# Seven products for eight in the projection of a hybrid recurrent layer

## The chip, the cores and the metric

The kernel runs on one core of a Trainium2 chip. Such a core has a matrix engine (TensorE, PE in the profile), a vector engine (VectorE, DVE), an engine for functions of one argument (ScalarE, ACT), a general one (GpSimd, POOL) and one that here only issues transfers (SyncE, SP). Each works through its own instructions in order; they meet at semaphores. Sixteen DMA engines move data between the memory of the device (DRAM) and the on-chip memory (SBUF); PE writes to accumulation banks (PSUM). The metric is the time on the device for one execution in microseconds, the median over runs.

## The reference

One layer over 2048 positions of width 1024. A normed and modulated input is projected to ten parts by one weight matrix of 1024 x 9216; two linear recurrences (HGRN2 and retention, 8 heads each) run on the parts; their normed outputs are gated, merged and projected back:

```python
h = rms_norm(x, norm_g[layer]) * (1.0 + scale) + shift
proj = h @ w_in[layer]
(hq, hf, hi, hz, rq, rk, rv, rz, ga, gb) = jnp.split(proj, offsets, axis=-1)
...
uA = head_rms_norm(oA, hg_norm_g[layer]) * jax.nn.silu(hz.astype(f32))
...
uB = head_rms_norm(oB, ret_norm_g[layer]) * jax.nn.silu(rz.astype(f32))
m = (jax.nn.sigmoid(ga.astype(f32)) * uA + jax.nn.sigmoid(gb.astype(f32)) * uB).astype(x.dtype)
x = x + gate * (m @ w_out[layer])
return rms_norm(x, final_g)
```

oA is the HGRN2 of hq, hf, hi: a state of 128 x 128 a head, with a decay that differs for each channel and position. oB is the retention of rq, rk, rv, whose q and k of 64 channels a head are rotated by position (rotary). All is in 32-bit floats.

## The kernel before

The positions go in two superblocks of 1024 (NSB = 2), the heads in four pairs (NP = 4). For each superblock and pair the function do_pair runs groups of products: "a" (f and q of the HGRN2, `gf` and `gq`, channels on the partitions), "b" for every second pair (q and k of the retention, `gr`, positions on the partitions), "c" (the values v of both, `gv`, positions on the partitions; they stay in SBUF as they are) and, for each of the two heads, "d" (`gg`: the four gate parts). Each group sums over the 1024 input channels in eight steps; each step is three matmuls of 128 x 128 x 512, since a 32-bit factor is split into a high and a low part and low times low is left out (mm3):

```python
PE.matmul(out=ps, lhsT=lh[0], rhs=rh[0], start=first, stop=False)
PE.matmul(out=ps, lhsT=lh[0], rhs=rh[1], start=False, stop=False)
return PE.matmul(out=ps, lhsT=lh[1], rhs=rh[0], start=False, stop=last)
```

All matmuls are issued at line 53, all transposes of PE at line 57, and PE keeps the order in which the program is written. Nothing is held from group to group but the split activations h (eight tiles for each block of 512 positions) and the weights: the class Ring loads a raw tile of two steps (L482, L480, on SP), splits it with ACT (the high part, L494) and DVE (the low part, L495) into one of 9 places (RING), 288 such splits in all.

Between the dense matmuls the recurrences run as generators in the class Background: after at least 9 steps of dense work (GAP) it lets each lane run one burst of small matmuls. The HGRN2 works with a tree over chunks of 16, 32, 64 .. 512 positions (`lv`, `poh`), the retention in chunks of 128 (`rt`, `por`). The q and k of the retention are rotated by DVE (L779, L793, L794), turned (L796) and sent through DRAM. normed (L706, L120, L121, L709) norms an output over its head; merge (L898, L901, L903) multiplies it with the gates (gates: L885, L888, L889), adds the two recurrences, turns the sum and stores it to mT_dram (L908).

startup works on h and the first v products at once. The last stage reads mT_dram, splits it (L1051, L1052), multiplies with the output weights (`ops`, 768 matmuls; load_wo, L1029 to L1031) and norms (L1239 to L1257). Which instruction of DVE, ACT, POOL and SP comes when is set by a scheduler that goes by dependences and priorities; only PE's order is the program's.

## Time and profile before

| what | us |
|---|---|
| median of 2 runs | 2048.34 |
| the two runs | 2047.32 and 2049.36 |
| the profiled execution, its own time and its span | 2048.5 |
| PE busy | 2029.8 |
| DVE busy | 1067.8 |
| ACT busy | 603.1 |
| POOL busy | 141.9 |

The span is the time from the first to the last instruction of the profiled execution; the profile gives no other time of that execution. An engine's busy time counts its arithmetic, not its issuing of transfers and its waits. Matmuls are pipelined and overlap in the record, so that a row's mean of one matmul is longer than the time it adds; that time is read where many follow each other without a gap. The DMA share is the mean busy share of the 16 DMA engines. A row of a window gives, for each engine, busy time and in brackets the instructions, then the clock that was granted to PE (1.00 is full), the DMA share and the rate in GB/s.

### The profile page before, as it was taken

To read this page: it belongs to the slowest core of one execution; us is meant where nothing else is said; L and a number is where in the kernel's file an instruction comes from. 1 tells how busy PE (TensorE), PEld (TensorE's weight loads), DVE (VectorE), ACT (ScalarE), POOL (GpSimd) and SP (SyncE) were. 2 spreads that over 40 slices of the span, in tenths; PEclk is the share of its full clock that TensorE was granted. 3 is DMA by queue.
4 is the path that set the end of the run, shared out by engine and by line. 5 is a ranking of instruction groups with operands and counts; after the bars stand their busy time and mean duration, and the time that the engine had idled before them with its cause. 6 is when DMAs were issued, how large, how long until landed. Compare 5 with 4: busy or idle time off the path is not lost.

```text
span 2048.5 us, 38333 instructions
## 1 busy us (share of the span) xinstructions
PE 2029.8 (99%) x15480; PEld 1672.5 (82%) x15480; DVE 1067.8 (52%) x2411; ACT 603.1 (29%) x1443; POOL 141.9 (7%) x246
## 2 busy tenths in 40 slices
PE   8999999999999999999999999999999999999998
PEld 6788888888888888888888888888878887888887
DVE  7376634553465535557465535553555535568432
ACT  7412222322114222436123212322123222323431
POOL 1000100110001100120000100010000100010000
PEclk9999999999999999999999999999999999999999
DMA  8135321322344211334334211321333211337541
GB/s 321 42 80 130 81 54 53 90 59 51 75 119 103 63 48 54 99 107 142 80 93 99 66 50 55 88 61 50 89 94 100 68 47 54 88 108 215 191 134 62
DMA packets 312562, 187.67 MB, mean 92 GB/s; under 512 B 217664, under 2 KB 274496, under 8 KB 312384
## 3 DMA queue, kind: packets, MB, share of 16 engines
q1 hardware_dynamic: 312384, 185.22, 32.9%
q8 instruction: 121, 1.98, 0.4%
q14 instruction: 57, 0.47, 0.1%
HBM read 147.39 MB, written 37.75 MB: 90 GB/s over the span
## 4 chain that ended last, share of the span: by engine, by line
PE 95%; DMA 2%; DVE 1%; ACT 1%; issue 0%; SPq 0%; POOL 0%; POOLq 0%; DVEq 0%; ACTq 0%
PE gg L53 34%; PE gv L53 16%; PE ops L53 9%; PE gq L53 9%; PE gf L53 8%; PE gr L53 8%; PE poh L53 4%; PE lv L53 3%; PE por L53 3%; PE rt L53 2%; DMA wc<-in_w_c_dram 1%; DVE wlc L495 0%; DMA bad<-in_bada_t_dram 0%; DVE wa L189 0%; DMA wd<-in_w_d_dram 0%
## 5 line engine op out<-in xcount | busy, mean ns | idle before, releaser
L53 PE MATMUL gg<-whd,h 128*128 128x512 f32 x2048 | 655.5, 394 | 0.0
L53 PEld LDWEIGHTS gg<-whd,h 128*128 128x128 f32 x2048 | 384.8, 188 | 77.9 <-issue 0.2
L53 PE MATMUL gg<-wld,h 128*128 128x512 f32 x1024 | 398.7, 389 | 0.0
L53 PE MATMUL gv<-whc,h 128*128 128x512 f32 x1024 | 330.4, 399 | 2.0 <-ACT h L393 1.9
L53 PEld LDWEIGHTS gv<-whc,h 128*128 128x128 f32 x1024 | 191.2, 189 | 43.6 <-ACT h L393 4.2
L53 PEld LDWEIGHTS gg<-wld,h 128*128 128x128 f32 x1024 | 192.6, 188 | 37.2 <-issue 0.2
L53 PE MATMUL gv<-wlc,h 128*128 128x512 f32 x512 | 194.3, 392 | 0.7 <-DVE wlc L495 0.7
L53 PE MATMUL gr<-whb,h 128*128 128x512 f32 x512 | 160.0, 391 | 0.0
L53 PE MATMUL ops<-wo,mh 128*128 128x512 f32 x512 | 157.9, 390 | 0.0
L53 PE MATMUL gq<-h,wha 128*128 128x512 f32 x512 | 157.7, 389 | 0.0
L53 PE MATMUL gf<-h,wha 128*128 128x512 f32 x512 | 157.6, 389 | 0.0
L885 ACT ACTIVATE sgg<-gg 128x512 f32<-128x512 f32 x128 | 75.5, 596 | 241.8 <-PE gg L53 241.3
L121 POOL TENSOR_TENSOR rrr<-ssr,mhalf 128x2 f32<-128x2 f32 x64 | 54.5, 851 | 1198.0 <-DVE ssr L120 1085.5
L495 DVE TENSOR_TENSOR wld<-wd,whd 128x512 fp32r<-128x512 f32 x128 | 86.3, 685 | 63.7 <-ACT whd L494 60.8
L53 PEld LDWEIGHTS gv<-wlc,h 128*128 128x128 f32 x512 | 96.6, 189 | 21.3 <-DVE wlc L495 2.2
L53 PEld LDWEIGHTS ops<-wo,mh 128*128 128x128 f32 x512 | 96.1, 188 | 20.3 <-DVE wo L1031 0.2
L53 PEld LDWEIGHTS gr<-whb,h 128*128 128x128 f32 x512 | 96.1, 188 | 20.0
L53 PEld LDWEIGHTS gf<-h,wha 128*128 128x128 f32 x512 | 96.1, 188 | 19.9
L53 PEld LDWEIGHTS gq<-h,wha 128*128 128x128 f32 x512 | 96.0, 188 | 19.8
L494 ACT ACTIVATE whd<-wd 128x512 fp32r<-128x512 f32 x128 | 79.2, 629 | 105.2 <-DMA wd<-in_w_d_dram 62.7
L888 DVE TENSOR_TENSOR ga<-gg,sgg 128x256 f32<-128x256 f32 x128 | 52.7, 415 | 94.0 <-ACT sgg L885 91.4
L53 PE MATMUL gr<-wlb,h 128*128 128x512 f32 x256 | 99.6, 389 | 0.0
(165 smaller groups left out, 2754.3 us busy)
## 6 DMA issues: line engine op xcount, KB each, us to landing
wd<-in_w_d_dram SPq DMA_DIRECT2D x64, 512.0 KB, 3.7
wc<-in_w_c_dram SPq DMA_DIRECT2D x32, 512.0 KB, 3.9
wa<-in_w_a_dram SPq DMA_DIRECT2D x32, 512.0 KB, 3.7
wa<-in_w_ada_dram SPq DMA_DIRECT2D x16, 512.0 KB, 7.6
wb<-in_w_b_dram SPq DMA_DIRECT2D x32, 256.0 KB, 3.2
qkT<-tr SPq DMA_DIRECT2D x128, 64.0 KB, 1.9
rqk<-qkT SPq DMA_DIRECT2D x64, 128.0 KB, 2.4
dk<-f SPq DMA_DIRECT2D x16, 512.0 KB, 2.8
```

What stands on the lines that cost most here:

```text
L53: made = nc.tensor.matmul(**kw)
L121: G.tensor_tensor(out=dst, in0=ss, in1=mhalf.broadcast_to([P, width]), op=ALU.pow)
L494: S.activation(out=hi, in_=w, func=AF.Copy)
L495: self.lasts.append(V.tensor_tensor(out=lo, in0=w, in1=hi, op=ALU.subtract).ins)
L885: S.activation(out=sg, in_=ps, func=AF.Sigmoid)
L888: V.tensor_tensor(out=ga, in0=ps[:, 0:256], in1=sg[:, 0:256], op=ALU.mult)
```

## The change

The projection is written anew. Columns go in quads: two blocks of 128 columns times two blocks of 512 positions, both with the two halves of the input channels; that is a product of 2 x 2 blocks, and Strassen's scheme (in Winograd's form) makes it of seven block products in place of eight. A quad is "a" (f, q of one head), "v" (the two v of one head), "b" (q and k of two heads of the retention), "A" or "B" (the gates of one); 36 for each superblock, 72 in all, and each product has 4 x 3 matmuls: 84 for a quad, 96 before.

- Activations: seven combinations of each of four channel blocks (A11, A12, A22, S1 to S4), split, are held in SBUF as 28 tiles. Those of the second superblock are made in the background by next_h, kept in DRAM and put in place by change_h around quad 36.
- Weights: four raw tiles are loaded for a quad, and one more that is summed up from step to step; the sums are made by DMAs that add to their destination, issued on POOL (Weights.add, L397, 4 for a quad, 288 in all). Each of the seven is split as before (L303 on ACT, L304 on DVE; 504 in all) into one of 3 places.
- Folds: after(m, q) takes the products' sums from PSUM: three copies by ACT (stash, L474) and three sums by DVE (L487 after product 1, L494 after 6, L498 after 7) for a quad. Products 1, 6, 7 and 4 of a quad use one bank after each other, 5 and 3 another; between two of these lies one other product (product_order).
- All ten parts come out with channels on the partitions. So both v are turned (take_v: L582 on DVE, then L587 to DRAM, read back at L826 and L914), the outputs of the recurrences are turned on their way back (L809, DRAM, L1005), the gates go through DRAM (L674, L1003), the merge follows there (L1015, L1018), and the rotation reads tables that tables() turns through DRAM at the beginning (L604 to L618: 128 transfers of 16 KB).
- The tree works on one head (NC = 8), the GAP is 8; normed squares on ACT; the states and norms go through DRAM as well. The opening computes the first two products of three quads while the combinations are made. The output stage is as before.

The core of the diff (new functions with a plus, the old product with a minus):

```diff
-    def mm3(ps, lh, rh, first, last):
-        PE.matmul(out=ps, lhsT=lh[0], rhs=rh[0], start=first, stop=False)
-        PE.matmul(out=ps, lhsT=lh[0], rhs=rh[1], start=False, stop=False)
-        return PE.matmul(out=ps, lhsT=lh[1], rhs=rh[0], start=False, stop=last)
...
-    def group_tok(sb, key, c, nm):
-        ps = dense_ps(f"{nm}_{sb * CH + c}")
-        for kt in range(KT):
-            tok_step(sb, key, c, ps, kt)
-        return ps
...
+def product_order():
+    made = [(5, 0), (3, 0)]
+    for i in range(NQ):
+        nxt = i + 1
+        if i + 1 < FIRST:
+            made += [(6, i), (5, nxt), (7, i), (3, nxt), (4, i)]
+        elif i < FIRST:
+            made += [(6, i), (2, nxt), (7, i), (5, nxt), (4, i)]
+        elif i + 1 < NQ:
+            made += [(1, i), (3, i), (6, i), (2, nxt), (7, i), (5, nxt), (4, i)]
+        else:
+            made += [(1, i), (3, i), (6, i), (7, i), (4, i)]
+    return made
...
+    def combine(h11, h12, h21, h22, use):
+        use("A11", h11)
+        use("A12", h12)
+        use("A22", h22)
+        V.tensor_tensor(out=h22, in0=h21, in1=h22, op=ALU.subtract)
+        use("S1", h22)
+        V.tensor_tensor(out=h21, in0=h11, in1=h21, op=ALU.subtract)
+        use("S3", h21)
+        V.tensor_tensor(out=h11, in0=h22, in1=h11, op=ALU.subtract)
+        use("S2", h11)
+        V.tensor_tensor(out=h12, in0=h12, in1=h11, op=ALU.add)
+        use("S4", h12)
...
+        def add(self, t, q, b, nm):
+            if ADMA:
+                nc.gpsimd.dma_start(out=as_src(t), in_=wsrc(q, b), accum_op=ALU.add)
+            else:
+                w = tmp(f"wt{nm}")
+                nc.sync.dma_start(out=as_src(w), in_=wsrc(q, b))
+                V.tensor_tensor(out=t, in0=t, in1=w, op=ALU.add)
...
+        def split(self, t):
+            m, q = seq[self.nsplit]
...
+            self.parts[m, q] = t
+            if m in (1, 2, 3, 7):
+                self.rfree += 1
+            elif m == 4:
+                self.zfree += 1
+                del self.z[q]
+            else:
+                self.add(src, q, 3 if m == 5 else 2, f"{m}n_{q}")
+            self.nsplit += 1
+            self.load()
...
+    def product_step(ps, m, q, j, first, last):
+        sb = QUADS[q][0]
+        at = combos[sb, ACOMBO[m], j]
+        bt = W.parts[m, q]
+        at_j = j % 2 * 2 + j // 2
+        ls = [z[:, at_j * P : (at_j + 1) * P] for z in bt]
+        for n, (x, y) in enumerate(((0, 0), (0, 1), (1, 0))):
+            PE.matmul(
+                out=ps, lhsT=ls[x], rhs=at[y], start=first and n == 0, stop=last and n == 2,
+                skip_group_check=True,
+            )
...
+    def stash(nm, ps):
+        t = upool.tile([P, 512], F32, name=nm, tag="cc", bufs=NCC)
+        S.activation(out=t, in_=ps, func=AF.Copy)
+        return t
...
+    def after(m, q):
+        with tc.high_priority(offset=PEV):
+            if m == 2:
+                c2s[q] = stash(f"c2_{q}", yb.pop(q))
+                return
+            if m == 5:
+                c5s[q] = stash(f"c5_{q}", vb[q])
+                return
+            if m == 1:
+                t = c2s.pop(q)
+                V.tensor_tensor(out=t, in0=xb[q], in1=t, op=ALU.add)
+                got = (0, 0, t)
+            elif m == 3:
+                c5s[q, 3] = stash(f"c53_{q}", vb.pop(q))
+                return
+            elif m == 6:
+                t = c5s.pop((q, 3))
+                V.tensor_tensor(out=t, in0=t, in1=xb[q], op=ALU.subtract)
+                got = (1, 0, t)
+            elif m == 7:
+                t = c5s.pop(q)
+                V.tensor_tensor(out=t, in0=t, in1=xb[q], op=ALU.subtract)
+                got = (1, 1, t)
+            else:
+                got = (0, 1, xb.pop(q))
+        deliver(q, *got)
...
+    def product(i):
+        m, q = seq[i]
+        if m == 2:
+            ps = yb[q] = bank(f"y{q}", xtag(q))
+        elif m == 1:
+            ps = xb[q] = bank(f"x{q}", xtag(q))
+        elif m == 5:
+            ps = vb[q] = bank(f"v{q}", "v")
+        elif m == 3:
+            ps = vb[q]
+        else:
+            ps = xb[q]
+        W.pump(i + NBW)
+        for j in range(4):
+            product_step(ps, m, q, j, m in (1, 2, 5) and j == 0, j == 3)
+            bg.tick(1.0)
+        W.parts.pop((m, q))
+        after(m, q)
...
+    def take_v(sb, h, s, tb, z):
+        y = tmp(f"vt{s}_{h}_{sb}_{tb}")
+        V.transpose(out=y, in_=z)
...
+                nc.sync.dma_start(out=t, in_=y)
+        yield
+        for b in range(L // BLK):
+            for i in range(2):
+                yield
+                for g in range(4):
+                    t = turned[i][(g // 2) * i]
+                    for j in range(4):
+                        nc.sync.dma_start(
+                            out=rot[i, b][32 * g : 32 * g + 32, :].rearrange("d (c j a) -> j d c a", j=4, a=32)[j],
+                            in_=t[32 * j : 32 * j + 32, b * P : (b + 1) * P].rearrange("d (c a) -> d c a", a=32),
+                        )
...
+    def opening():
+        was = {0: ada_load(0)}
+        scb = row_of_c()
+        W.load()
...
+        lower_bounds()
+        late_consts()
+        for _ in tables():
+            pass
+        for q in range(FIRST):
+            after(2, q)
+            if q == 0:
+                after(1, q)
```

In the opening, SP's order before has the weights of the next groups one after the other; names are destination and source, and `w` with a letter is a raw weight tile:

```order
L482 DMA wa_1_661<-in_w_a_dram 128x1024
L482 DMA wa_2_667<-in_w_a_dram 128x1024
L482 DMA wa_3_703<-in_w_a_dram 128x1024
L480 DMA wb_0_739<-in_w_b_dram 128x2x256 x2
L93 DMA m_802<-in_msk_dram 128x66
L480 DMA wb_1_789<-in_w_b_dram 128x2x256 x2
L480 DMA wb_2_1029<-in_w_b_dram 128x2x256 x2
L480 DMA wb_3_1046<-in_w_b_dram 128x2x256 x2
L482 DMA wd_0_1063<-in_w_d_dram 128x1024
L482 DMA wd_1_1079<-in_w_d_dram 128x1024
```

Now the tables (`rot`, from the turned tables `tabd`) stand there, and behind them the raw weight of product 5 of the third quad (`wz`), then those of its product 7 and of the fourth quad:

```order
L618 DMA rot_1_312<-tabd_0_811 128x1x32 x16
L618 DMA rot_1_316<-tabd_0_817 128x1x32 x8
L618 DMA rot_1_316<-tabd_1_820 128x1x32 x8
L618 DMA rot_2_313<-tabd_0_811 128x1x32 x16
L618 DMA rot_2_317<-tabd_0_817 128x1x32 x8
L618 DMA rot_2_317<-tabd_1_820 128x1x32 x8
L618 DMA rot_3_314<-tabd_0_811 128x1x32 x16
L618 DMA rot_3_318<-tabd_0_817 128x1x32 x8
L618 DMA rot_3_318<-tabd_1_820 128x1x32 x8
L419 DMA wz_1052<-in_w_b_dram 128x4x128
L411 DMA w_2_1058<-in_w_b_dram 128x4x128
L411 DMA w_3_1060<-in_w_d_dram 128x4x128
```

The 128 transfers of the tables have come in ahead of `wz`; 96 of them stand in these rows, the others in front.

On PE at that place the order is now as follows; x, y, v with a number are the banks of that quad, b5_2 the split weights of product 5 of quad 2 (counted from 0):

```order
L82 MATMUL x0_521<-A22_0_2_676,b4_0_1049 128x512 x3
L82 MATMUL x0_521<-A22_0_3_753,b4_0_1049 128x512 x3
L82 MATMUL x1_523<-S2_0_0_513,b6_1_1082 128x512 x3
L82 MATMUL x1_523<-S2_0_1_603,b6_1_1082 128x512 x3
L82 MATMUL x1_523<-S2_0_2_688,b6_1_1082 128x512 x3
L82 MATMUL x1_523<-S2_0_3_765,b6_1_1082 128x512 x3
L82 MATMUL v2_1153<-S1_0_0_505,b5_2_1100 128x512 x3
L82 MATMUL v2_1153<-S1_0_1_595,b5_2_1100 128x512 x3
L82 MATMUL v2_1153<-S1_0_2_680,b5_2_1100 128x512 x3
L82 MATMUL v2_1153<-S1_0_3_757,b5_2_1100 128x512 x3
```

Product 5 of quad 2, whose raw weight is that `wz`, is the ninth product after the opening's six, so 14 x 12 = 168 dense matmuls stand ahead of it.

In the middle of the first superblock PE had, in a group of v, steps of three matmuls with a burst of small ones between:

```order
L53 MATMUL gv3_2_7753<-whc120_7296,h0_0_217 128x512
L53 MATMUL gv3_2_7753<-wlc120_7297,h0_0_217 128x512
L53 MATMUL gv3_2_7753<-whc120_7296,h0_0_217 128x512
L53 MATMUL rt3_1_7761<-rqk3_1_7511 128x128 x2
L53 MATMUL rt3_1_7761<-v3_0_7724,rkz3_0_7508 64x128 x2
L53 MATMUL lv3_0_2_7771<-q3_0_7318,k3_0_7317 32x16 x64
L53 MATMUL por3_0_0_7764<-v3_0_7724,scm3_0_7647 128x128
L53 MATMUL por3_0_1_7765<-v3_0_7724,scm3_0_7647 128x128
L53 MATMUL gv3_2_7753<-whc121_7548,h0_1_259 128x512
L53 MATMUL gv3_2_7753<-wlc121_7549,h0_1_259 128x512
```

Now, around the gates quad 21, PE goes from product 2 of quad 22 to product 7 of quad 21, to product 5 of quad 22, to product 4 of quad 21:

```order
L82 MATMUL y22_6666<-A12_0_3_750,b2_22_6620 128x512 x3
L82 MATMUL x21_6577<-S3_0_0_509,b7_21_6640 128x512 x3
L82 MATMUL x21_6577<-S3_0_1_599,b7_21_6640 128x512 x3
L82 MATMUL x21_6577<-S3_0_2_684,b7_21_6640 128x512 x3
L82 MATMUL x21_6577<-S3_0_3_761,b7_21_6640 128x512 x3
L82 MATMUL poh4_0_6705<-vh4_0_0_6248,k4_0_5619 128x128
L82 MATMUL poh4_0_6705<-vh4_0_0_6248,af_113 128x128
L82 MATMUL v22_6718<-S1_0_0_505,b5_22_6667 128x512 x3
L82 MATMUL v22_6718<-S1_0_1_595,b5_22_6667 128x512 x3
L82 MATMUL v22_6718<-S1_0_2_680,b5_22_6667 128x512 x3
L82 MATMUL v22_6718<-S1_0_3_757,b5_22_6667 128x512 x3
L82 MATMUL x21_6577<-A22_0_0_501,b4_21_6689 128x512 x3
```

A product is 12 matmuls now, and the same bank `x21` is used by products 6, 7 and 4 with one product of the other quad between.

DVE before has at a like place, among the gates of head 4, splits, gates and merges of 256 and 128 columns:

```order
L756 SCALAR_TENSOR_TENSOR st5_114<-st5_114,tl2_0_6446,poh2_4_6834 128x128
L495 TENSOR_TENSOR wld109_6862<-wd13_2_6796,whd109_6861 128x512
L709 SCALAR_TENSOR_TENSOR v2_4_6118<-poh2_4_6834,rrh2_4_6844,gh0_2_5600 128x128 x2
L898 TENSOR_TENSOR ga4_4_6724<-ga4_4_6724,v2_4_6118 128x256
L495 TENSOR_TENSOR wld110_6878<-wd13_3_6822,whd110_6877 128x512
L901 TENSOR_TENSOR ga4_4_6724<-ga4_4_6724 128x128
L495 TENSOR_TENSOR wld111_6888<-wd13_3_6822,whd111_6887 128x512
L903 STREAM_TRANSPOSE ga4_4_6724<-ga4_4_6724 128x128
L888 TENSOR_TENSOR ga4_6_6905<-gg4_6_6784,sgg4_6_6903 128x256
L889 TENSOR_TENSOR ga4_6_6905<-ga4_6_6905,sgg4_6_6903 128x256
L888 TENSOR_TENSOR ga4_7_6910<-gg4_7_6785,sgg4_7_6908 128x256
L889 TENSOR_TENSOR ga4_7_6910<-ga4_7_6910,sgg4_7_6908 128x256
```

Now the fold L498 of quad 21 comes behind rotations of quad 20 (`ct`, `sw`), turning, gates (`c2_21`) and splits; between the fold L494 of that quad and the first row here stand eleven others, three of a merge (L1015 twice, L1018), six of rotation, a transpose and a split:

```order
L630 TENSOR_TENSOR sw1_2_1_6491<-c5_20_6177,sn1_2_1_6490 64x512
L632 TENSOR_TENSOR ct1_2_1_6489<-ct1_2_1_6489,sw1_2_1_6491 128x512
L634 STREAM_TRANSPOSE sw1_2_1_6491<-ct1_2_1_6489 128x512
L629 TENSOR_TENSOR sw0_2_1_6570<-x20_6260,sn0_2_1_6569 64x512
L630 TENSOR_TENSOR sw0_2_1_6570<-x20_6260,sn0_2_1_6569 64x512
L631 TENSOR_TENSOR ct0_2_1_6568<-x20_6260,ct0_2_1_6568 128x512
L661 TENSOR_TENSOR c2_21_6468<-c2_21_6468,sz0_4_0_6617 128x512
L632 TENSOR_TENSOR ct0_2_1_6568<-ct0_2_1_6568,sw0_2_1_6570 128x512
L673 TENSOR_TENSOR c2_21_6468<-c2_21_6468,c53_21_6638 128x512
L562 MEMSET f5_0_7006 128x2
L304 TENSOR_TENSOR b4_21_6689<-wz_21_6158,b4_21_6689 128x512
L498 TENSOR_TENSOR c5_21_6549<-c5_21_6549,x21_6577 128x512
```

Three folds a quad have come in, each of which a product of PE waits for.

1459 lines of the change are left out of this document (695 added, 764 removed).

## Prediction

> **What bounds the kernel now.** I read the page from the top: busy shares, the slices, the queues, the summary of the chain. After that I asked for the chain in order of time, and for windows.
>
> ```profile
> span 2048.5 us, 38333 instructions
> PE 2029.8 (99%) x15480; PEld 1672.5 (82%) x15480; DVE 1067.8 (52%) x2411; ACT 603.1 (29%) x1443; POOL 141.9 (7%) x246
> ...
> PE   8999999999999999999999999999999999999998
> ...
> DVE  7376634553465535557465535553555535568432
> ...
> PEclk9999999999999999999999999999999999999999
> DMA  8135321322344211334334211321333211337541
> ...
> q1 hardware_dynamic: 312384, 185.22, 32.9%
> ...
> PE 95%; DMA 2%; DVE 1%; ACT 1%; issue 0%; SPq 0%; POOL 0%; POOLq 0%; DVEq 0%; ACTq 0%
> ```
>
> TensorE (PE) is busy for 2029.8 of 2048.5 us, in nearly every slice to the top digit and at a full clock; the chain that ended last is 95% PE. Vector (DVE) stands at half, the DMA engines at a third. So a matmul that is taken out is worth its own duration, as long as no other engine comes late. The profiled execution took 2048.5 us, the median shown is 2048.34: the sum below is made against 2048.5 and needs no correction.
>
> What one dense matmul costs shows in the chain's last long piece, the output stage with nothing between its matmuls (start, duration, what):
>
> ```profile
> 1867.46 174.14 PE ops L53 x768
> ```
>
> 174.14 / 768 = 0.2267 us. (The page's mean of 394 ns for one instruction overlaps its neighbours.) A window of 100 us in which hardly anything but dense matmuls ran gives 100 / 440 = 0.227 too, with DVE at 46 us and the DMA engines at 0.34:
>
> ```profile
> 1400.00:1500.00 100.00, 99.52 (x440) 82.02 (x438) 46.49 (x92) 18.86 (x32) 0.00 (x0) 1.00 0.34 94
> ```
>
> **The change part by part.**
>
> *Products.* 6912 projection matmuls become 72 quads x 84 = 6048; the 768 of the output stage stay, and so do the small ones of the recurrences. -864 x 0.2267 = -195.9 us. The time that PE spends on dense work before is 7680 x 0.2267 = 1741 us; 2029.8 - 1741 - 10 (transposes and warm-up matmuls of the opening) = 279 us is the small work, which I carry over.
>
> *Vector work.* These rows give a price for each new kind (columns: line, engine, operation, tiles, shapes, count | busy us, mean ns | idle before):
>
> ```profile
> L495 DVE TENSOR_TENSOR wld<-wd,whd 128x512 fp32r<-128x512 f32 x128 | 86.3, 685 | 63.7 <-ACT whd L494 60.8 <-PE lv L53 2.8
> ...
> L898 DVE TENSOR_TENSOR ga<-ga,v 128x256 f32<-128x256 f32 x128 | 53.1, 417 | 1.2
> ...
> L796 DVE STREAM_TRANSPOSE tr<-qk 128x512 f32<-128x512 f32 x32 | 22.7, 710 | 0.8
> ...
> L1239 DVE TENSOR_TENSOR xo<-xo,ops 128x512 f32<-128x512 f32 x32 | 22.0, 686 | 54.1 <-PE ops L53 54.1
> ...
> L189 DVE CUSTOM_DVE_ANT_0 wa<-wa,scb,bad 128x1024 f32<-128x1024 f32 x16 | 20.2, 1281 | 2.1 <-DMA wa<-in_w_ada_dram 2.0
> ...
> L1255 DVE SCALAR_TENSOR_TENSOR xo<-xo,or,fgs 128x512 f32<-128x512 f32 x16 | 12.0, 752 | 10.7 <-POOL or L1253 10.7
> ...
> L494 ACT ACTIVATE whd<-wd 128x512 fp32r<-128x512 f32 x128 | 79.2, 629 | 105.2 <-DMA wd<-in_w_d_dram 62.7 <-PE gv L53 18.6 <-PE gg L53 17.5
> ```
>
> Splits: 504 instead of 288 at 0.685 (the new tile has 512 columns as well), +148 us. Folds, the sums of the products: 213 of 128x512 from PSUM, nearest the row of L1239 with 0.686, +146. Turning v and the outputs: 128 transposes at 0.71 (row L796), +91. Combinations of the activations, 32 x 0.685 = 22, and some 15 us net of rotation, gates and merge (the 128x256 merges of L898, 0.417, become 64 of 128x512, which I put at L1255's 0.752, and adds). Sum 1068 + 422 = 1490 us, about 75% of the new span. On the average that fits; DVE is in order, though, and each quad makes PE wait for three folds: product 6 writes over what L487 reads, product 7 over what L494 reads, product 4 over what L498 reads. Between lies one product of 12 matmuls, 2.7 us, which is four DVE instructions. DVE's order, whose end at this place is shown above, has 23 instructions after L494 up to L498 of quad 21, the gates quad behind a quad of retention q and k: 3 merges (2 x 0.752 + 0.685), 2 transposes (1.42), 17 others of 0.685 (11.6) and a short one, 15.3 us. PE has there products 2 of the next quad, 7, and 5 of the next quad, 36 x 0.2267 = 8.2 us, and little small work: about 7 us of waiting. There are 8 such places (one for each such quad) and the change of the activations in the middle; a part of each is caught by PE running behind DVE (one product). Bounds: 0 if the fold is always ahead, 8 x 7 + some 30 at the other quads = 86; I take 40 us, since most of the other quads have DVE work for 10 to 20 us against 20 to 23 us of PE. ACT gets 216 more splits and 213 stashes at 0.629 (its row L494), +270 us on 603 before gates and squares: half of the span, and a stash has a whole product to be done in, so I cost it at nothing; if ACT were late, the next to wait is PE at the bank of products 5 and 3.
>
> *Clock after a wait.* The trace has one wait in mid-stream, 2.26 us at 1705:
>
> ```profile
> 1705.00:1710.00 5.00, 2.74 (x90) 2.25 (x79) 2.73 (x4) 0.36 (x1) 0.00 (x0) 0.90 0.21 75
> 1710.00:1715.00 5.00, 5.00 (x18) 4.03 (x17) 2.68 (x5) 0.00 (x0) 0.00 (x0) 0.75 0.00 0
> 1715.00:1720.00 5.00, 5.00 (x155) 4.00 (x155) 2.29 (x4) 1.34 (x5) 0.00 (x0) 1.00 0.15 43
> ```
>
> The granted clock is 0.90 and 0.75 in two windows of 5 us and then 1.00 again: (0.10 + 0.25) x 5 = 1.75 us lost. Eight waits like it: 14 us; none and 50 are the bounds.
>
> *The opening.* Before, PE computes v of the first pair from the start:
>
> ```profile
> 0.00:20.00 20.00, 4.10 (x17) 3.10 (x18) 0.00 (x0) 1.00 0.90 350
> 20.00:40.00 20.00, 15.78 (x61) 10.59 (x60) 0.00 (x0) 1.00 1.03 409
> 40.00:60.00 20.00, 18.61 (x73) 12.76 (x72) 2.28 (x4) 1.00 0.24 65
> 60.00:80.00 20.00, 12.15 (x46) 7.59 (x44) 2.26 (x4) 1.00 0.35 107
> ```
>
> That is 17 + 61 + 73 + 46 = 197 dense matmuls in 80 us, and by then PE is full. Afterwards nothing dense runs until the activations' combinations exist. On DVE these need 16 x 1.281 (L189) + 28 splits x 0.685 + 16 combinations x 0.685 + 6 weight splits and the row of c, about 8 us: 20.5 + 19.2 + 11.0 + 8 = 59 us, which begin at some 5 us, so 64 us. Meanwhile PE has 72 matmuls. Then the rotary tables: L618 issues 128 DMAs of 16 KB, all on SP, and behind them on SP stands the load of the raw weight of product 5 of the third quad (L419), which PE reaches after 168 dense matmuls. The DMAs of 16 KB that before has (minimum, median, maximum of an issue in ns):
>
> ```profile
> L908 SPq DMA_DIRECT2D mT_dram<-ga x512: 302/430/1967, 207.3 to 1878.9; - x171
> ...
> DMA to landing us min/median/max: 1.4/1.5/4.5
> ```
>
> 128 x 0.43 = 55 us (0.302 would give 39, the 0.604 of the row below 77). 64 + 55 + 4 for the two tables = 123 us; then the load:
>
> ```profile
> L480 SPq DMA_DIRECT2D wb<-in_w_b_dram x32: 539/604/684, 69.1 to 1446.5; - x32
> ...
> DMA to landing us min/median/max: 3.0/3.2/3.9
> ```
>
> 3.2 us, as much for the accumulating DMA behind it, 1.3 for the split and some latency: PE goes on at about 132 us, with 6048 + 768 - 168 = 6648 dense matmuls before it: 6648 x 0.2267 = 1507, + 279 small, + 8 for the tail (the last outputs are turned and merged through DRAM; before, the tail behind PE is 7): 1926 us. If the tables were hidden, PE would go on from 72 matmuls at 70 us: 70 + 6744 x 0.2267 + 279 + 8 = 1886. Their only cover are weights loaded before them, and there are three raw tiles and two for sums.
>
> *Accumulating DMAs.* 288 of 256 KB in pieces of 512 bytes, issued by POOL. Before issues none from POOL and adds nothing in flight: their price isn't in the trace. The plain load of the same size (L480, just above) lands in 3.2 us, and by the code an accumulate has about three products, 8 us, from its issue to its split, so I cost its latency at nothing; at twice 3.2 us it is still covered. On POOL's queue the powers of the output norms (L181) now stand behind adds that wait for their load; what waits for those are outputs on their way to the merge, for which PE waits only at the end, so nothing again; as issues, 288 at the 0.604 of L480 are 174 us on a POOL that is busy for 142. For the engines' load I take two rows: in the opening the DMA engines are full and move 409 GB/s,
>
> ```profile
> 15.00:20.00 5.00, 4.94 (x25) 3.67 (x24) 4.96 (x10) 2.50 (x5) 0.00 (x0) 1.00 1.03 410
> 20.00:40.00 20.00, 18.05 (x81) 12.97 (x80) 17.66 (x37) 17.06 (x35) 1.66 (x1) 1.00 1.03 409
> ```
>
> so 1.03 x 16 / 410 = 0.0402 ns a byte and engine; on the page the mean packet has 185.22 MB / 312384 = 593 bytes and takes 0.329 x 2048.5 x 16 / 312384 = 34.5 ns, so 10.7 ns are fixed. The changed kernel moves 423 MB in 865 thousand packets (its 360 + 288 weight transfers, and v, outputs, gates, tables through DRAM): (865e3 x 10.7 + 423e6 x 0.0402) / 16 = 1640 us of each engine, 83% of 1985, if an accumulating packet costs what a copy costs. Bounds: that, and three times that. If counted twice, 147456 packets x 31.3 ns / 16 = 288 us come on top, 1930 in all. I take the copy's price, with the rest as rivals. SP's queue has 2269 issues for 1252, at 0.43 some 976 us, half of the span.
>
> **Sum.** 132 + 1507 + 279 + 8 = 1926, + 40 for folds + 14 for the clock = 1980; the change of the activations in the middle (28 splits within seven products, DVE 31 us against PE 26) adds 5: 1985 us.
>
> **The rivals.**
> 1. Stalls hidden: the folds come in time and the tables hide partly. 1886 to 1930. For it: DVE at 75% leaves room. Against: the 23 instructions at each of eight places.
> 2. The DMA engines become the bound, each accumulating packet costing two. 1930 us of work on engines that can't be full in the opening (66 us idle or so) and at the tail: 2000 to 2080, say 2045, no measurable change. For it: 83% by the copy's price leaves little. Against: nothing in the rows but that weights are loaded in time at 33%. The mechanism is that an add reads its destination as well as its source. The Trainium skill states this in "Collectives: The Full Stack", section "The bandwidth ceiling: the fold count and why AG ≠ RS ≠ AR": an add in the DMA path needs two source reads, and the reduce ran at half the rate of the copy. No run here shows it yet.
> 3. Slower: PE waits at each of the 216 folds. Place: L487, L494, L498, behind whatever DVE has in hand. Price: 1945 without stalls; two DVE instructions ahead of each beyond the 2.7 us cover, 1.37 x 216 = 296, give 2240; it decides from 0.67 us a fold, (2089 - 1945) / 216, one instruction. For it: DVE itself waits for ACT and PE in its order (before, L495 has 63.7 us of such waits in 128). Against: folds are emitted with a priority that moves them ahead.
> 4. Accumulating packets at three prices: 1640 + 577 = 2217 us of each engine, so 2250, slower. It takes over 2.4 prices to matter.
>
> **How the numbers follow.** About 2% is what a measurement of this kernel can tell from no change: faster is below 2007, slower above 2089. Chances: the forecast's case 0.36 (1930 to 2007), rival 1 0.12, rival 2 0.18 and larger stalls that stay within 2% 0.08, rival 3 0.18, rival 4 0.08. So faster 0.48, same 0.26, slower 0.26. The likeliest case gives 1985. The range from 1915 to 2130 leaves out half of rival 1 (0.06) and what of rivals 3 and 4 lies above (0.14); the forecast's own range is 1930 to 2007.
>
> **What would show it.** In the profile after: the mean of a dense matmul in the chain's output piece still 0.227; PE empty in slices 2 and 3, with SP's queue in L618 until about 123 us; DVE at 1450 to 1530 us; folds as the releaser of PE's idle time with about 40 us, at gates quads above all; PEclk below 9 only after such waits; the DMA share at 0.80 to 0.85 (1 would be rival 2 or 4, with PE or the split waiting for the accumulating DMAs). Wrong would be a PE idle time spread evenly over quads (rival 3), or waits for POOL's queue, whose issues no row of before prices.

## The result, and the profile after

The changed kernel takes 2655.81 us (median of 2651.90 and 2659.71) for 2048.34: a ratio of 1.2964, 95% interval 1.2916 to 1.3012. It is slower by 30%. The profiled execution's span is 2650.1 us.

The page of the changed kernel, the lines that answer to those of before (busy times, three rows of slices, the DMA queues, the chain by engine):

```profile
span 2650.1 us, 40994 instructions
PE 1998.0 (75%) x14648; PEld 1584.5 (60%) x14648; DVE 1365.1 (52%) x2647; ACT 937.6 (35%) x2340; POOL 618.2 (23%) x674
...
PE   4526997499856887488774998399857888497998
...
PEclk9758998799987998798887999699988899798999
DMA  8347787668776798699885788668786778577753
...
q1 hardware_dynamic: 752720, 348.08, 49.9%
q0 software_dynamic: 152064, 75.52, 23.6%
...
PE 16%; DMA 8%; DVE 4%; SPq 3%; issue 3%; POOL 1%; ACT 1%; POOLq 0%; DVEq 0%; ACTq 0%
```

PE does fewer products and yet is busy for 1998.0 us, at a mean clock below full, and stands idle for 652 us; the chain no longer runs along PE (16%) but through transfers, DVE, SP's queue and others, in pieces of a few microseconds. What PE waited for (microseconds in all, times, the longest):

```profile
PE y L82 <- DVE ct L631: 231.8, 7, 39.9
PE v L82 <- ACT b L303: 73.4, 6, 70.1
PE poh L82 <- DMA vh<-vd: 53.7, 10, 9.7
PE rt L82 <- DMA rqk<-rd: 46.1, 9, 11.2
...
PE poh L82 <- DMA k<-dk: 27.4, 7, 12.9
...
PE x L82 <- DVE c L487: 14.8, 13, 3.6
...
PE x L82 <- DVE c L498: 12.2, 6, 4.2
...
PE x L82 <- DVE c L494: 6.5, 6, 1.8
```

The folds, L487, L494 and L498, which the prediction had as the whole of the waiting, make 33.5 us. Seven waits for a row of the rotation, L631, make 231.8. Windows of the opening and of the stretch from there to the last part of the output stage (PE busy, PE's loads, DVE, ACT, POOL, granted clock, DMA share, GB/s):

```profile
0.00:200.00 200.00, 83.44 (x430) 59.95 (x431) 82.64 (x164) 68.63 (x114) 30.13 (x39) 0.77 0.53 128
200.00:2540.00 2340.00, 1811.40 (x13766) 1439.49 (x13765) 1240.17 (x2402) 838.17 (x2158) 582.07 (x624) 0.89 0.77 165
```

So PE is idle for 117 us in the first 200 and for 529 us after, at a mean clock of 0.77 and 0.89. Against the 1985 us forecast: in PE's timeline the 70 us wait of the opening ends at 183 us and not at 132 (+51); idle time after it is 529 us for 40 (+489); and the busy time of PE exceeds the 2029.8 - 195.9 = 1834 us of full clock by 164, for 14 (+150). Together 690, a little more than the 671 that are missing: PE's work in the opening at a slow clock is counted in two of them.

**One of the seven long waits, link by link.** PE's timeline (start, duration; in brackets the idle time before) at the retention quad 20 and the gates quad 21, the place whose order the prediction had counted:

```profile
770.41 2.94 PE L82 MATMUL x<-S,b 128*128 128x512 f32 x12
813.30 5.28 PE L82 MATMUL y<-A,b 128*128 128x512 f32 x12 [39.95 <-DVE ct L631]
```

The second row is product 2 of quad 22. It writes to the bank that quad 20 used last (the code gives even quads the bank x0), and there the rotation still has to read product 4 (L631 reads `x20`). DVE's timeline before that:

```profile
773.39 0.69 DVE L494 TENSOR_TENSOR c<-c,x 128x512 f32<-128x512 f32 x1 [0.92 <-PE x L82]
777.29 0.75 DVE L1015 SCALAR_TENSOR_TENSOR mg<-mg,gnt,mu 128x512 f32<-128x512 f32 x1 [3.21 <-DMA mu<-ud]
779.04 0.75 DVE L1015 SCALAR_TENSOR_TENSOR mg<-mg,gnt,mu 128x512 f32<-128x512 f32 x1 [1.00 <-DMA mu<-ud]
...
786.47 0.69 DVE L631 TENSOR_TENSOR ct<-c,ct 128x512 f32<-128x512 f32 x1 [2.47 <-DMA ct<-rot]
796.09 0.69 DVE L304 TENSOR_TENSOR b<-wz,b 128x512 fp32r<-128x512 f32 x1 [8.93 <-ACT b L303]
...
811.04 0.68 DVE L629 TENSOR_TENSOR sw<-x,sn 64x512 f32<-64x512 f32 x1 [11.37 <-DMA sn<-rot]
...
812.47 0.69 DVE L631 TENSOR_TENSOR ct<-x,ct 128x512 f32<-128x512 f32 x1
```

The fold L494 is done at 774. Then DVE waits in its row for a load of the merge (3.2 and 1.0 us), for a table (2.5), for a split's high part (8.9) and for another table (11.4), and L631 comes at 812.5: 39 us, of which some 27 are waiting. SP's issues in that time show why the loads were late:

```profile
752.91 0.61 SPq L1005 DMA_DIRECT2D mu<-ud  x1
765.36 1.13 SPq L639 DMA_DIRECT2D rd<-ct  x2
766.53 5.31 SPq L1005 DMA_DIRECT2D mu<-ud  x3
771.88 1.52 SPq L1003 DMA_DIRECT2D mg<-gd  x1
773.45 3.61 SPq L1005 DMA_DIRECT2D mu<-ud  x4
...
778.31 0.67 SPq L419 DMA_DIRECT2D wz<-in_w_d_dram  x1
...
798.95 1.07 SPq L639 DMA_DIRECT2D rd<-ct  x2
800.12 6.20 SPq L644 DMA_DIRECT2D kzd<-sw  x4
806.36 1.64 SPq L627 DMA_DIRECT2D ct<-rot  x1
808.05 0.43 SPq L628 DMA_DIRECT2D sn<-rot  x1
```

SP stands from 753.5 to 765.4 in the store L639 until DVE has rotated; behind it stand the merge's loads (L1005), behind these the table and the next `wz` (778.31). POOL waits for that weight and issues its adding transfer at 783.72 (below), and only at 795.4, 11.7 us later, can ACT split it. That split is what DVE waits 8.9 us for, so this link is the time of two transfers as well as SP's order. Until the split is made DVE doesn't finish the next rotation, and SP, standing in the store L639 of that rotation, issues nothing from 791.2 to 798.95. Behind that store the four stores L644 take 6.2 us to issue, and the last table (L628, 808.05) stands behind them. Two queues, each in order, wait for each other in turn. The DMA engines were not full: their share is 0.82 from 780 to 792, 0.15 from 792 to 800 and 0.60 from 800 to 812. POOL's row:

```profile
783.72 1.44 POOL L397 DMA_DIRECT2D wz<-in_w_d_dram  x1 [15.31 <-DMA wz<-in_w_d_dram]
```

DVE has the same four waits in the same order (merge load, table, split, table) ahead of the waits of PE that end at 531, 1438, 1725 and 2296; the one at 1997 has the last two of them, and the shortest, at 1112, another (a load of x, 12.4 us).

### The profile page after: what moved, and what is told of

Same layout as the page of the kernel before. It is cut to its first block, busy times and chain, and to the rows that moved or that the text cites. A ratio compares the mean times of both kernels' runs of the same rounds, so it can differ in the third digit from the quotient of the medians.

```text
span 2650.1 us, 40994 instructions
## 1 busy us (share of the span) xinstructions
PE 1998.0 (75%) x14648; PEld 1584.5 (60%) x14648; DVE 1365.1 (52%) x2647; ACT 937.6 (35%) x2340; POOL 618.2 (23%) x674
## 3 DMA queue, kind: packets, MB, share of 16 engines
q0 software_dynamic: 152064, 75.52, 23.6%
## 5 line engine op out<-in xcount | busy, mean ns | idle before, releaser
L82 PE MATMUL v<-S,b 128*128 128x512 f32 x1728 | 455.8, 409 | 88.3 <-ACT b L303 73.4
L82 PE MATMUL x<-S,b 128*128 128x512 f32 x1704 | 440.1, 403 | 25.7 <-DVE c L487 14.8
L82 PE MATMUL x<-A,b 128*128 128x512 f32 x1704 | 431.7, 403 | 20.7 <-DVE c L498 12.2
L82 PE MATMUL y<-A,b 128*128 128x512 f32 x852 | 248.4, 441 | 252.7 <-DVE ct L631 231.8
L82 PEld LDWEIGHTS v<-S,b 128*128 128x128 f32 x1728 | 332.6, 197 | 166.8 <-ACT b L303 76.8
L82 PEld LDWEIGHTS x<-S,b 128*128 128x128 f32 x1704 | 322.1, 193 | 103.2 <-ACT b L303 15.6
L82 PEld LDWEIGHTS x<-A,b 128*128 128x128 f32 x1704 | 322.7, 193 | 92.9 <-ACT b L303 9.4
L304 DVE TENSOR_TENSOR b<-w,b 128x512 fp32r<-128x512 f32 (+1 forms) x320 | 200.3, 635 | 257.5 <-ACT b L303 254.1
L304 DVE TENSOR_TENSOR b<-wz,b 128x512 fp32r<-128x512 f32 (+1 forms) x240 | 150.4, 636 | 309.6 <-ACT b L303 308.7
L397 POOL DMA_DIRECT2D wz<-in_w_d_dram x96 | 149.5, 1585 | 495.9 <-DVE b L304 338.7
L303 ACT ACTIVATE b<-w 128x512 fp32r<-128x512 f32 (+1 forms) x320 | 183.2, 584 | 189.2 <-PE x L82 82.0
L303 ACT ACTIVATE b<-wz 128x512 fp32r<-128x512 f32 (+1 forms) x240 | 137.5, 583 | 223.2 <-DMA wz<-in_w_b_dram 71.3
L82 PE MATMUL ops<-wo,m 128*128 128x512 f32 x768 | 179.7, 394 | 8.1 <-ACT m L303 4.7
L474 ACT ACTIVATE c<-v 128x512 f32<-128x512 f32 x144 | 85.7, 595 | 146.6 <-PE v L82 146.3
L397 POOL DMA_DIRECT2D wz<-in_w_a_dram x48 | 80.5, 1678 | 135.0 <-DVE b L304 85.4
L474 ACT ACTIVATE c<-y 128x512 f32<-128x512 f32 x71 | 42.3, 596 | 177.5 <-PE y L82 177.3
```

Source lines behind the costliest of these rows:

```text
L82: return tc.keep_in_program_order(nc.tensor.matmul(**kw))
L303: S.activation(out=t[0], in_=src, func=AF.Copy)
L304: return V.tensor_tensor(out=t[1], in0=src, in1=t[0], op=ALU.subtract)
L397: nc.gpsimd.dma_start(out=as_src(t), in_=wsrc(q, b), accum_op=ALU.add)
L474: S.activation(out=t, in_=ps, func=AF.Copy)
```

## The experiments

Each time is that of one execution; the kernel before, run beside them on the same chip, took 2047.9 to 2052.6. Differences are against 2655.8, whose two runs are 7.8 us apart; less than that is called no gain.

### Single links

**a1_copy.** Plain copies for the adding transfers:

```diff
-                nc.gpsimd.dma_start(out=as_src(t), in_=wsrc(q, b), accum_op=ALU.add)
+                nc.gpsimd.dma_start(out=as_src(t), in_=wsrc(q, b))
```

> The 288 transfers that add to their destination become plain copies of the same size from the same queue (POOL); the sums of the weights are left out. Theory SP (SP's single queue brings weights and rotary tables late): the time stays within 60 us of 2656, since the order and the issues are the same. Theory DMA (an adding packet costs two copies, so the DMA engines hold everything up): the queue of POOL falls from 23.6% of 2650 us to about 11%, landing from 6 us to about 3.5, and the time falls by 200 us or more.

2558.7 us, 97 less: between the two. POOL's queue on its page (packets, MB, share of 16 engines):

```profile
q0 software_dynamic: 23040, 75.52, 10.5%
```

0.105 x 2556.9 x 16 = 4296 us of engine time for the same 75.52 MB that cost 0.236 x 2650.1 x 16 = 10007 us when added: 2.3 times, or 65.8 ns for each of 152064 packets. The share is as theory DMA had it, and landing fell from 5.9 to 4.3 us in the median; the time is not as it had it: the waits for L631 are still 195 us. The edit changes more than the adding: the copies go in larger packets (23040 for 152064), and POOL issues one in 0.88 us for 1.45.

**a2_rot_act.** Loads of the tables from ACT (`nc.scalar.dma_start` at L627 and L628):

> The 64 loads of the rotary tables (L627, L628) are issued by ACT, not by SP. Theory SP order (the fourth load of a retention quad waits on SP behind the stores L644): the seven waits of the bank y for L631, 232 us, fall to under 80 and the time by 150 us or more. Theory tiles (the load waits for its place, whatever the queue): the waits stay within 60 us of 232 and the time within 60 of 2656.

2634.3, 22 less. The waits for L631 fell to 126 us, but 63 us for the tree's k through DRAM (27 before) and others came in their place. The fall of the waits lies between the two theories; the time is that of the second.

**a3_stash.** The fourth sum copied out of PSUM:

```diff
-                got = (0, 1, xb.pop(q))
+                z = xb.pop(q)
+                if QUADS[q][1] == "b":
+                    z = stash(f"c4_{q}", z)
+                got = (0, 1, z)
```

> ACT copies the fourth sum of a retention quad out of PSUM, so that the bank is free without DVE. Theory bank (the wait is for the bank alone): the 232 us of waits for L631 vanish, and the time falls by 200 us or more. Theory SP (DVE stands in its row behind a late table, and the folds behind it): the wait for L631 vanishes but comes back at L498 or at a split within two or three products; the time falls by 100 us at most.

2660.2, no gain. The bank is free, and PE waits at the same places a few rows later, for the tree's k, not at the fold or the split that the second theory named:

```profile
PE poh L82 <- DMA k<-dk: 208.4, 8, 35.9
```

So the bank is where the delay shows, not where it is made.

**a4_weights_act.** Weights loaded from ACT (`nc.scalar.dma_start` at L411 and L419):

> The 360 plain loads of weights (L411, L419) are issued by ACT, not by SP. Theory SP (weights are late because they stand behind the tables and the outputs on SP): the first long wait, 70 us at 113, falls to under 20, the waits for splits shrink, and the time falls by 150 us or more. Theory DMA (the engines are the bound): the time stays within 60 us of 2656. Against a gain: 360 x 0.6 us more on ACT's row.

2651.9, no gain; the waits for L631 are 240 us. The first long wait of 70 us went, but one of 55 for a turned v (L582) came just behind it. The first theory had the wait right and the time wrong. The second has the time, but the engines' load is not the whole of the loss either: a1_copy takes it down and gains 97 us.

**a5_tables.** Half of the tables later:

```diff
+            if b == NBLK:
+                yield "rest"
...
-        for _ in tables():
-            pass
+        tab = tables()
+        for said in tab:
+            if said == "rest":
+                break
+        bg.side.append(tab)
```

> In the opening only the 64 transfers of the rotary tables that the first superblock needs are issued; the other 64 come from the background later. Theory SP in the opening (the 70 us wait is the queue of tables ahead of the third quad's weights, 88 us for 128): the wait falls by 40 us or so, to about 27, and the time by 40 to 60. Theory other (the wait is for the sum that POOL makes, or for the split): the wait stays within 10 us of 70.

2657.0, no gain, but the scheduler had moved most of the later transfers up again. SP's row of the tables, of the kernel as changed and of this one:

```profile
93.50 80.08 SPq L618 DMA_DIRECT2D rot<-tabd  x122
```

```profile
95.51 70.26 SPq L620 DMA_DIRECT2D rot<-tabd  x106
```

16 fewer stood ahead of `wz`, and the wait fell from 70.1 to 60.2 us: 0.62 us for each. That fits a wait for the queue of tables, most of which the edit hadn't taken away; c1_tables32 below settles it.

**a7_bstores, a8_stores.** Stores of rotated q and k, and then all stores of results, from ACT (`nc.scalar.dma_start` at L639 and L644; at L587, L674, L784, L812, L883 and L1022 as well):

> The stores of the rotated q and k (L639, L644) are issued by ACT, the loads stay on SP. Theory convoy (SP and DVE are two queues in order that wait for each other: SP stands in a store until DVE has rotated, DVE stands in a row until SP has issued the load behind that store): the seven long waits, 232 us, fall to under 90 and don't come back elsewhere; the time falls by 130 us or more. Theory DMA (the transfers of these stretches take that long on the engines): the waits stay over 170 us, the time within 60 us of 2656.

> All stores of results to DRAM (L587, L639, L644, L674, L784, L812, L883, L1022, some 580 issues) are issued by ACT. Theory convoy: beside the long waits those for v and the rotated q and k (L826, L911, 100 us) shrink to about half; the time falls by 250 us or more. Against: ACT gets 350 us of issues in front of its splits; if that costs more than SP gains, the splits (L303) become PE's releaser and the time stays above 2560.

2604.1 and 2605.2, 52 and 51 less. The waits for L631 fell to 130 and 79, but with all stores on ACT the tree's k made 91 us and `lv` 42 us of new ones. Convoy's sign, but 52 where it had 130 or more, and 51 where it had 250 or more. The splits on ACT did not become what PE waits for (74 us, nearly all in the opening).

**a6_dve_add.** Sums on DVE:

```diff
-ADMA = True
+ADMA = False
```

> The sums of the weights are made on DVE from plain loads, with no adding transfers. DVE gets 288 x 0.685 = 197 us more, SP 288 issues. Theory DMA: the DMA share falls from 0.75 to about 0.62 and the time by 100 us or more. Theory convoy (more loads on SP and more rows on DVE make the waiting worse): the time rises by 100 us or more.

2616.9, 39 less, with the DMA share at 0.60. Neither theory. The waits for L631 fell to 106 us, but behind the opening PE waited 87 for splits on ACT (8 in the kernel as changed). So part of the gain went into later weights; whether DVE's longer row (1538 us) or SP's 288 more loads delayed them isn't shown.

### Several together

**b1_three.** The edits of a1_copy, a8_stores and a3_stash in one kernel.

> Three single edits together: plain copies for the adding transfers (the weights' sums are left out), all stores of results from ACT, and the fourth sum of a retention quad copied out of PSUM. Alone they gave 97, 51 and 0 us (2558.7, 2605.2, 2660.2 for 2655.8). Theory chain (a long wait is a row of links one behind the other, in queues that are in order: a link taken out gains its own length only, and the wait moves to the next): the gains add, about 150 us, 2500 to 2530. Theory bank and queue as single causes, hidden by each other: over 250 us.

2538.8, 117 less, where the single gains sum to 148. That is 9 us short of the chain's 2500 to 2530 and far from the 250 us of the other theory: the gains nearly add, and of these three none hid a large one.

**b2_no_rot, b3_rows.** Rotation without loads, and turned transfers in whole rows (shown for L1005; L587, L644 and L777 likewise):

```diff
-        nc.sync.dma_start(out=ct, in_=rot[0, b])
-        nc.sync.dma_start(out=sn, in_=rot[1, b])
+        sn = tb1 = combos[sb, "A11", 0][0]
```

```diff
-                        out=ut[32 * i : 32 * i + 32, :].rearrange("e (c j t) -> e c j t", c=4, j=4),
-                        in_=ud[s, h, b].rearrange("(j e) (c i t) -> i e c j t", j=4, c=4, i=4)[i],
+                        out=ut[32 * i : 32 * i + 32, :],
+                        in_=ud[s, h, b][32 * i : 32 * i + 32, :],
```

> The rotation reads a resident tile in place of its loaded tables (so q and k of the retention are not rotated); DVE's rows stay, 64 loads and two of twelve places in the ring of working tiles go. Theory loads of tables (the fourth load behind the stores sets the wait): the seven waits, 232 us, fall under 60, nothing takes their place, time 200 us or more lower. Theory chain: the wait is cut by the 14 us that the profile shows for the two loads in the stretch at 773 (2.5 and 11.4), the rest stays at a split or at k<-dk; the time falls by 80 to 150 us.

> The turned transfers (v, k of the retention, the tree's k, the outputs: L587, L644, L777, L1005) move whole rows of 2 KB in place of pieces of 128 bytes, as many issues and bytes, so that their results are not turned. Theory pieces (360 thousand of 905 thousand packets are these pieces; they fill the DMA engines and SP's issues): packets fall below 560 thousand, the DMA share from 0.75 to about 0.6, SP's issues of 1.4 to 1.8 us to 0.6, and the time by 150 us or more. Theory chain: the share falls likewise, but the time only by 50 to 100 us.

2566.6 (89 less, the chain's band, though the waits for this row of the rotation fell to 45 us: 78 for the tree's k and 44 for splits took their place) and 2470.2 (186 less, the largest single gain, in time the band of pieces). The second kernel's packets:

```profile
DMA packets 567067, 426.21 MB, mean 173 GB/s; under 512 B 59472, under 2 KB 469072, under 8 KB 566864
```

Only 59 thousand are under 512 bytes, for 420 thousand in the kernel as changed, while the DMA share fell just from 0.74 to 0.72 of a shorter span, not to 0.6; the store L644 took 0.48 us to issue in the median, for 1.41. So the gain is of the pieces, but whether through the engines or through SP's issues stays open. The seven waits for L631 are 159 us there.

**b4_all.** The edits of b2_no_rot, b3_rows and a1_copy in one kernel.

> Whole rows, plain copies and no table loads together (the weights' sums, the turning and the rotation are left out). PE, ACT and DVE keep their rows. Theory DMA (all that is lost is lost to transfers: their number, their adding, their place in the queue): the time falls to 2150 or less. Theory vector row (PE waits for DVE in its order even when transfers are quick): 2300 or more, with L487, L494, L498 and the splits as PE's releasers.

2354.7, 301 less where the three single gains sum to 372. Over the 2300 of the second theory, but not by its folds: besides the 69 us of the opening, PE's largest waits are 73 us for the tree's k and 39 for the retention's state (L957), both of the recurrences. So I asked what is left without them.

### The projection alone, the opening, a kernel with all that helped

**c2_core, c4_core_copy.** What a quad delivers is dropped but for a part of A; in the second kernel the adding transfers are copies too:

```diff
+        if kind == "A" and ch == 0:
+            if tb:
+                z = stash(f"c4_{q}", z)
+            nc.sync.dma_start(out=mT_dram[b][n], in_=z)
+            msent[n, b] = bg.now
...
-        if kind == "a":
-            take_a(sb, n, ch, tb, z)
```

> The recurrences, gates, turning and merge are left out: what a quad delivers is dropped, but for two parts of each quad A that are stored for the output stage. The opening, the weights with their adding transfers, splits, folds, the change of the activations and the output stage stay: 6816 dense matmuls, 1545 us. Theory recurrences (the projection keeps up by itself): 183 for the opening + 6648 x 0.2267 = 1690, + 10 for the tail, so 1690 to 1760, with PE at over 95% from 200 us on. Theory weights (the three places, the adding transfers and the folds are too slow by themselves): over 1850, with the splits as PE's releaser.

> As the kernel before it in this list, with plain copies in place of the adding transfers (the weights' sums left out too). Theory recurrences: within 20 us of that kernel. Theory weights: at least 60 us faster than it.

1759.0, the upper end of the first theory's range and 59 over its sum without waits, and 1734.8: the projection, with its folds, splits and adding transfers, nearly keeps up by itself. Page and a window of the first:

```profile
PE 1598.3 (91%) x6904; PEld 1308.4 (74%) x6904; DVE 684.0 (39%) x1131; ACT 582.0 (33%) x1075; POOL 449.9 (26%) x354
```

```profile
1000.00:1100.00 100.00, 100.00 (x443) 82.81 (x442) 36.08 (x58) 31.34 (x58) 30.67 (x22) 1.00 0.73 132
```

From 200 to 1700 us PE is busy for 1470 of 1500; in steady stretches 443 matmuls in 100 us, 0.226 us each, with the DMA engines at 0.73. The adding transfers cost 24 us here, a little more than the first theory's 20.

**c1_tables32.** Tables in 32 transfers (each for all four blocks):

```diff
-        for b in range(L // BLK):
...
+                        out=rot_all[i][32 * g : 32 * g + 32, :].rearrange("d (c j a) -> j d c a", j=4, a=32)[j],
+                        in_=t[32 * j : 32 * j + 32, :].rearrange("d (c a) -> d c a", a=32),
```

> The rotary tables are turned by 32 transfers of 64 KB in place of 128 of 16 KB; all else stays. Theory SP in the opening (in a5 the wait fell by 10 us with the 16 transfers that left the queue, 0.65 us each): 32 x 0.7 to 1.4 = 22 to 45 us on SP instead of 88, the wait of 70 us falls to 5 to 30, and the time by 45 to 65 us. Theory other: the wait stays within 10 us of 70.

2593.2, 63 less. The wait in the opening:

```profile
PE v L82 <- ACT b L303: 15.5, 5, 13.3
```

**c3_best.** The edits of c1_tables32, a8_stores and a3_stash, and `nf <= n + 2` for `nf <= n + 1` in the HGRN2's fetch of v.

> Everything is computed. Tables in 32 transfers, all stores of results from ACT, the fourth sum of a retention quad copied out of PSUM, and v of the HGRN2 fetched one chunk earlier. Theory chain (links add): 55 + 51 + 0 + 35, so about 2515. If the links hide each other: 2400 or less. It is not expected to reach the kernel before the change.

2544.5, 111 less than the kernel as changed, with everything computed. The parts sum to 114 (63 + 51 + 0) if the earlier fetch of v gave nothing. It doesn't reach the kernel before; no variant that computes everything did.

### One recurrence at a time

**d1_hgrn, d2_ret.** What the quads of one recurrence deliver is dropped (shown for the first):

```diff
+        if kind in ("b", "B"):
+            return
...
+        if s == 1:
+            return
```

> The retention is left out: its rotation, tables, v, gates and chunks; merge takes the HGRN2's part alone. The projection's products all stay. Theory retention (the long waits at the quads of q and k, the tables and its chunks make most of the loss): 1759 + 150 of small matmuls - 63 for the opening's tables + 100 or so, under 2000. Theory meeting (either alone is carried, both together aren't): under 2050 here and under 2150 with the retention alone, the two additions together at least 200 us less than the 897 of both. Theory HGRN2: over 2250.

> The HGRN2 is left out: f, q, tree, its v, gates and chunks; merge takes the retention's part alone. Theory retention: 2250 or more, with the long waits for L631 as before. Theory meeting: under 2150, and the seven long waits of 33 us shrink, since what stands in DVE's and SP's rows between the folds is fewer. Theory HGRN2: under 1950.

| us | without HGRN2 | with HGRN2 |
|---|---|---|
| without retention | 1759.0 | 1970.3 |
| with retention | 2197.3 | 2655.8 |

With the HGRN2 alone PE's waits are 158 us in all, opening included; with the retention alone the long waits stand at the same quads:

```profile
PE y L82 <- DVE ct L635: 146.0, 7, 29.0
```

The kernel without retention has no tables either; with the 63 us that these cost in c1_tables32, the HGRN2 adds 1970.3 + 63 - 1759.0 = 274, the retention 438, both 897: 185 us come from their meeting (248 without that correction). The theories each have a part: the first kernel is under 2000 as the retention's theory had it, the second above the 2150 of meeting alone and below the 2250 of the retention alone; the long waits shrank from 33 to 21 us each. The recurrences' small matmuls are the 279 us of the prediction's sum, so some 620 of the 897 are loss. PE's busy time nearly adds (1598 us with neither, 1804 and 1773 with one, 1998 with both); its idle time doesn't (159 with neither, 165 with the HGRN2, which has no tables in the opening, 422 with the retention, 652 with both). So the meeting is mostly in waits, and the retention brings long waits even alone.

## Why the prediction was wrong

**Right.** The products: 864 fewer at 0.2267, and one in the output stage takes 0.2274 us now (103.68 us for 456). The price of an adding packet in rival 2: 65.8 ns, 2.1 times the 31.3 worked out for a copy of its size. The Trainium skill, "Collectives: The Full Stack", section "The bandwidth ceiling: the fold count and why AG ≠ RS ≠ AR", says of a collective's reduce that the add needs two source reads. The price here agrees with that; no run shows the reads themselves. The engines' load is 0.735 x 2650 = 1948 us, beside the 1930 that a doubled price gave. But it is no bound at 2656, and the projection alone runs at 0.226 us a matmul with it, so rivals 2 and 4 are not what happened.

**Right in number, by luck: the fold waits.** They are 33.5 us for 40, but not where the prediction had them: 25 waits of at most 4.2 us, and no wait of 7 us at a gates quad behind a retention quad. At quad 21 PE stands earlier, for the bank, and product 4 behind that doesn't wait for its fold.

**Wrong, the step that failed:** "each quad makes PE wait for three folds", taken as the whole of PE's new waiting after the opening, with loads and stores of the recurrences costed at nothing and the place at quad 21 at 7 us. There the wait is 40. I had counted DVE's rows, but with every load on time; the rows between L494 and L631 wait for 27 us for loads that come late: 18 of these for loads on SP behind stores that wait for DVE, 9 for a split whose adding transfer came late. And I let PE run product 2 of quad 22 freely, though DVE's order showed product 4 of quad 20 still being read by L631 in the same bank, seventeen rows behind L494. The single links tried (table loads, stores, bank, adding, sums on DVE) each gave 0 to 97 us and the wait moved on; the projection without recurrences came within 59 us of its sum. So what failed is the cover: data that stayed in SBUF before (v, the gates, the outputs) now pass through DRAM just in time, with some 2270 issues in one queue in order, of which a third (704) go in pieces of 128 bytes. That the greater part of the loss comes with the recurrences and what serves them is shown (1759 without them), but that kernel leaves out their vector rows and small matmuls along with their transfers. That transfers are the reason is shown for the 301 us that lighter and fewer ones gave (b4_all) and argued for the rest. Single sizes are shown for pieces (186 us in whole rows), stores (51) and table loads (22 moved, 89 left out); how the rest divides between landing times, issues and the order of the queues stays open.

**Wrong in size: the opening.** 183 us, not 132. The term was right in kind (SP's tables ahead of `wz`), shown by c1_tables32, where fewer transfers for the tables gave 63 us. Its issues took longer than the row of before that I used, as the row of L618 has it (minimum, median, maximum in ns, first and last start):

```profile
L618 SPq DMA_DIRECT2D rot<-tabd x128: 521/598/1454, 84.8 to 173.0; - x128
```

88 us from 84.8, not 55 from 68. DVE reached the turned table some 17 us later than summed: in the first 50 us a window has it busy for 24.3 only.

**Wrong in size: the clock.** PE's busy time is 164 us above that of full clock, for 14. Not all of it is the clock: PE's busy time in windows of 5 us, times what the clock lacks of 1.00, sums to some 110 us (2 before). The other 50 or so may be matmuls that end with none overlapping them; that isn't shown. I had multiplied one small wait's loss by eight; PE's timeline has 43 waits of more than 3 us, 513 us in all, and after long ones the clock is at half. Windows of 5 us at the end of the wait at 773 (PE busy is the second figure; the granted clock is the third from the end):

```profile
810.00:815.00 5.00, 1.70 (x4) 1.44 (x5) 3.88 (x7) 0.00 (x0) 0.00 (x0) 0.50 0.79 233
815.00:820.00 5.00, 5.00 (x16) 3.91 (x16) 0.23 (x1) 1.12 (x2) 0.00 (x0) 0.68 0.26 56
820.00:825.00 5.00, 2.54 (x14) 1.87 (x13) 2.13 (x4) 1.45 (x4) 0.00 (x0) 1.00 0.56 129
```

**Wrong in size, without weight:** DVE is busy for 1365 us, not 1490.

**The rivals.** Rival 3 had PE waiting at each fold, which it doesn't. None had what the seven long waits show: SP's and DVE's queues waiting for each other. Where the prediction counted SP's 2269 issues as half of the span, it should have asked what stands behind what.

## What to carry to other kernels

A sum of busy times and a count of rows tell whether an engine has the time, not whether its inputs are there: where results leave through the same queue in order by which inputs come, a store can wait for the engine and a load behind it make the engine wait. Before taking a transfer through DRAM as hidden, read the queue's order at one place and ask of each row what it waits for. When the wait moves on with each link that is taken out, leave a whole stage out and see what remains.

## What the runs showed of the hardware

- A transfer that adds to its destination cost 2.3 times the engine time of the copy of the same bytes from the same queue (10007 for 4296 us), and landed in 5.9 for 4.3 us in the median. It goes in 152 thousand packets of 0.5 KB, the copy in 23 thousand of 3.3 KB.
- The issue of one and the same store (L644, 64 KB in pieces of 128 bytes) took 0.33 us at least, 1.41 in the median and 3.81 at most on SP. From ACT it took 0.38 in the median (a7_bstores), and on SP in whole rows 0.48 (b3_rows). Why isn't shown. POOL's issue of an adding transfer took 1.45 us in the median, of a plain copy 0.88.
- After the wait of 40 us that ended at 813.3, PE's granted clock was 0.50 in every window of 1 us until 818, 0.89 in the next and 1.00 from 819: some 5 us of work at half.
